# A recurrent branch without GpSimd, and two selection rounds and two rows of a modulation moved by a stage

## The chip, the cores and the metric

The kernel runs on one core of a Trainium2 chip, as one program from inputs in HBM to outputs in HBM. The metric is device time in microseconds of that core, median of several runs. The engines are named as the profile names them: PE (matrix multiplication), DVE (vector), ACT (activations, and copies with scale and bias), POOL (GpSimd), SP (issues most of the DMAs). Each engine runs its own instruction list strictly in order, and semaphores tie the lists together.

## What is computed

Two blocks of a small model on 512 tokens of width 1024, in float32. Only the first block is touched. Cut to what matters:

```
proj = modulate(rmsnorm(h)) @ w_in                      # all projections
xr, gr, q, ckv, qi, ki, wi, mg = split(proj)
hr  = rg_lru(causal_dwconv(xr))                         # 10 blocks of 128 channels
  r, i = sigmoid(x @ w_a + b_a), sigmoid(x @ w_x + b_x)
  log_a = -8 * softplus(-lam) * r;   a = exp(log_a)
  inp = sqrt(-expm1(2 * log_a)) * (i * x)
  h_t = a_t * h_(t-1) + inp_t                           # scan over the tokens
y_a = (gelu(gr) * hr) @ w_rnn_out
sel = top_k(indexer scores, 128 keys for each query);  att = softmax over sel
y_b = att @ w_att_out
mix = (ga * y_a + gb * y_b) @ w_out                     # ga, gb = sigmoid(mg)
h = h + g1 * mix;  u2 = modulate(rmsnorm(h), sh2, sc2)
h = h + g2 * hier_moe(u2)                               # 32 experts
# g1, sh2, sc2, g2: four rows of 1024 of silu(c) @ w_mod + b_mod
```

## The kernel before

Activations are kept feature-major: a tile is 128 channels by 512 tokens. Float32 products are made of three passes on PE: each operand is split into a rounded part (a cast on ACT, L145) and the remainder (a subtraction on DVE, L146), and `mmk` issues high by low, low by high and high by high (L298, L299, L301). `FM.tile` loads 256 columns of a weight matrix (`raw`), splits them into `wh` and `wl`, and multiplies. A split thus needs ACT and then DVE before PE can begin.

A list scheduler decides the order of each engine's instructions from the order of the code, and `weave` interleaves the code of several generators: each is advanced in proportion to the number beside it. Tiles come from pools with a fixed number of buffers.

The stages of the first block that the change touches, with their place in the trace:

- The recurrence (86 to 306 us). `rg_lru` goes over ten blocks of 128 channels in five groups of two. `rg_first` computes the convolution (L691 on ACT, three L693 on DVE) and splits the result (`xcp`); `rg_gates` multiplies it by two gate matrices (`rga`, `rgx`) and multiplies the input gate by x on GpSimd (L709); `rg_decay` makes the decay `a` of a group and the factor of its input out of a sigmoid and a tanh (L717 to L730); `rg_last` applies the square root by one Newton step (L736 to L739), scans (L741), and multiplies by gelu(gr) into `gT`. Beside it run the scores of the key selection (`index_scores`, L623 on ACT and L626 to L630 on DVE) and the first 8 of 16 rounds of `top_k`: in each round and each of three query tiles, a maximum of eight (L636) and their replacement (L637), on DVE.
- Branch A (306 to 373 us): eight tiles of `gT` by `w_rnn_out`, beside the other 8 rounds of `top_k` and row 0 of the second modulation. A row (`mod_rows`) is eight loads of 512 KB, eight multiply-accumulates of 128x1024 on DVE (L802, L804), two small products on PE (L812) and two small additions.
- Attention (373 to 541 us), beside rows 1 to 3 and the last gates.
- Branch B (541 to 592 us): eight tiles of `att` by `w_att_out`, each multiplied by its gate on DVE (L977), added to branch A's on GpSimd (L978) and split into `mT`.
- Then the mix by `w_out`, routing (to 665 us), and the experts (665 to 1122 us), whose weights come by DMA.

Of the kernel before, what the change touches and what calls it, by code (L numbers as in the profile page):

```python
# [64 lines left out]
def build(ctx, tc, I, out, dbg=None):  # L65
# [20 lines left out]
    def weave(*streams):  # L86

        live = [[g, n, 0] for g, n in streams]
        while live:
            s = min(live, key=lambda e: e[2] / e[1])  # L90
            s[2] += 1
            try:
                next(s[0])
            except StopIteration:
                live.remove(s)

    def pipelined(n, score, out, steps=4):

        late = None
        for h in range(n + 1):
            for i in range(steps):
                if h < n:
                    score(h, i)
                if h:
                    products = out(h - 1, i)
                    rest = late and late()
                    late = products
                    if rest:  # L110
                        late = lambda a=rest, b=products: (a(), b())[1]
                yield
        while late:
            late = late()
# [50 lines left out]

    shiftc = const("shiftc", [128, 1])
    G.memset(shiftc, -SHIFT)

    def columns(specs, tag):
        rows = t_([128, 128], F32, "SG", f"rows{tag}")  # L170
# [428 lines left out]
    ps = trp("wit")  # L599
# [15 lines left out]
    def index_scores():  # L615
        for i in range(1, 4):
            n = 128 * (i + 1)
            a = sel[i]
            for h in range(8):
                ps = trp("idx")  # L620
                mm_stacked(ps[:, 0:n], qiT[h // 2], kiT[:, h % 2, 0:n], h % 2, slice(i * 128, (i + 1) * 128))
                rl = sa("rel", n)
                S.activation(rl, ps[:, 0:n], AF.Relu)  # L623
                w = wi[:, i * 8 + h:i * 8 + h + 1]
                if h == 0:
                    V.tensor_scalar(a, rl, w, None, OP.mult)  # L626
                else:
                    V.scalar_tensor_tensor(a, rl, w, a, OP.mult, OP.add)
                yield
            V.tensor_tensor(a[:, i * 128:n], a[:, i * 128:n], cmask, OP.add)  # L630

    def top_k(r0, r1):
        for r in range(r0, r1):
            for i in range(1, 4):
                m8 = sm("m8", 8)
                V.max(m8, sel[i])  # L636
                V.match_replace(sel[i], m8, sel[i], -3e38)  # L637
                yield
        if r1 == 16:
            for i in range(1, 4):  # L640
                V.tensor_scalar(sel[i], sel[i], -1e38, NEG, OP.is_gt, OP.mult)
# [57 lines left out]
    def rg_gates(b, w2, xc, y, keep):  # L699
        wh, wl = w2[:, 0], w2[:, 1]  # L700
        pr = trp("rga")
        mm3(pr, (wh[:, 0], wl[:, 0]), (xc[:, 0], xc[:, 1]), True, True)
        pi = trp("rgx")
        mm3(pi, (wh[:, 1], wl[:, 1]), (xc[:, 0], xc[:, 1]), True, True)
        tx = pt_("tx", F32)
        t, gx = tx[:, 0], tx[:, 1]
        S.activation(t, pr, AF.Sigmoid, bias=col["b_rg_a"][:, b:b + 1])
        S.activation(gx, pi, AF.Sigmoid, bias=col["b_rg_x"][:, b:b + 1])
        G.tensor_tensor(gx, gx, y, OP.mult)  # L709
        keep.append((b, t, gx))  # L710

    def rg_decay(keep):

        ap = pt_("ra", F32)
        for n, (b, t, gx) in enumerate(keep):
            a = ap[:, n]
            S.activation(a, t, AF.Sigmoid, bias=shiftc, scale=sp8[:, b:b + 1])  # L717
            S.activation(a, a, AF.Copy, bias=0.5, scale=0.5 * math.exp(SHIFT))
            S.activation(t, t, AF.Tanh, scale=sp4[:, b:b + 1])
            G.tensor_scalar(t, t, -1e-24, None, OP.min)  # L720
            rec = sg("rec")
            V.scalar_tensor_tensor(rec, t, 1.0, a, OP.subtract, OP.mult)
            V.scalar_tensor_tensor(rec, rec, 2.0, a, OP.add, OP.mult)
            V.tensor_scalar(a, rec, 2.0, -1.0, OP.mult, OP.add)
            G.tensor_tensor(gx, gx, rec, OP.mult)

        ys = []
        for b, t, gx in keep:
            y = sa("rsq")
            S.activation(y, t, AF.Abs_reciprocal_sqrt, scale=-0.25)  # L730
            ys.append(y)
        return [(b, ap[:, n], t, gx, ys[n]) for n, (b, t, gx) in enumerate(keep)]

    def rg_last(b, a, u, gx, y):

        G.tensor_tensor(u, u, y, OP.mult)  # L736
        V.tensor_tensor(y, u, y, OP.mult)
        V.scalar_tensor_tensor(u, y, 12.0, u, OP.add, OP.mult)
        V.scalar_tensor_tensor(gx, u, -1.0 / 16, gx, OP.mult, OP.mult)  # L739
        hs = sg("hs")  # L740
        V.tensor_tensor_scan(hs, a, gx, 0.0, OP.mult, OP.add)  # L741
        ps = fmg.tile(1280 + 128 * b)
        g2 = sg("g2")
        S.activation(g2, ps, AF.Square, scale=math.sqrt(0.044715))
        V.scalar_tensor_tensor(g2, g2, 1.0, ps, OP.add, OP.mult)
        S.activation(g2, g2, AF.Tanh, scale=math.sqrt(2.0 / math.pi))
        V.scalar_tensor_tensor(g2, g2, 1.0, ps, OP.add, OP.mult)
        V.tensor_tensor(g2, g2, hs, OP.mult)
        p = pg("gT")
        split(p[:, 0], p[:, 1], g2)  # L750
        gT.append(p)

    def rg_lru():
        prev = []
        for g in range(6):
            keep = []
            for n in range(2):
                if g < 5:
                    gates = rg_first(2 * g + n, keep)
                    yield  # L760
                    gate(2 * g + n)
                    yield
                if prev:
                    rg_last(*prev[n])
                    yield
                if g < 5:
                    gates()
            if g < 5:
                prev = rg_decay(keep)
                yield  # L770

    def chain(*gs):
        for g in gs:
            yield from g

    weave((rg_lru(), 36), (chain(index_scores(), top_k(0, 8)), 50))


    A_d = dr.tile([8, 128, 512], F32, name="A_d")
# [2 lines left out]
    def branch_a():  # L782
        for d in range(8):
            th = sg("ga")
            load(th, gate_d[d])
            pya = fmy.tile(128 * d)
            V.tensor_tensor(th, th, pya, OP.mult)
            load(A_d[d], th)
            yield
# [1 line left out]

    mod_d = dr.tile([4, 1024], F32, name="mod_d")

    def mod_rows(m0, m1):
        for m in range(m0, m1):
            a = pt_("macc", F32, (128, 1024))
            c0 = 2048 + m * 1024
            for k in range(8):
                raw = pg("raw", F32, (128, 1024))
                load(raw, w_mod[k * 128:(k + 1) * 128, c0:c0 + 1024])  # L800
                if k == 0:
                    V.tensor_scalar(a, raw, csil[:, 0:1], None, OP.mult)  # L802
                else:
                    V.scalar_tensor_tensor(a, raw, csil[:, k:k + 1], a, OP.mult, OP.add)  # L804
                if k % 2:
                    yield
            for hf in range(2):
                cs = slice(hf * 512, hf * 512 + 512)
                br = sg("bmr", 512)
                load(br[0:1, :], I["b_mod"][:, c0 + hf * 512:c0 + hf * 512 + 512])  # L810
                ps = trp("mrow")
                PE.matmul(ps[0:1, :], ones[:, 0:1], a[:, cs], start=True, stop=True)  # L812
                V.tensor_tensor(br[0:1, :], br[0:1, :], ps[0:1, :], OP.add)
                if m == 2:
                    ng = sg("n2g", 512)
                    load(ng[0:1, :], I["norm2_g"][:, cs])
                    V.scalar_tensor_tensor(br[0:1, :], br[0:1, :], 1.0, ng[0:1, :], OP.add, OP.mult)
                load(mod_d[m:m + 1, cs], br[0:1, :])
            yield

    weave((branch_a(), 8), (top_k(8, 16), 24), (mod_rows(0, 1), 6))


    columns(R2, "2")
# [138 lines left out]
            split(p[:, 0], p[:, 1], po)  # L963
            att.append(p)

    weave((pipelined(8, att_score, att_out), 36), (gate_b(), 6), (mod_rows(1, 4), 13))


    fmb = FM(I["w_att_out"][0], att, 0, 1024)
    mT = []  # L970
    for d in range(8):
        ps = fmb.tile(128 * d)
        a = sg("A")
        load(a, A_d[d])
        v = sg("mv")
        load(v, gate_d[8 + d])
        V.tensor_tensor(v, v, ps, OP.mult)  # L977
        G.tensor_tensor(v, v, a, OP.add)  # L978

        p = pg("mT")  # L980
        hi, lo = (p[:, n].rearrange("p (c r) -> p r c", r=8) for n in range(2))
        split(hi, lo, v.rearrange("p (r c) -> p r c", r=8))
        mT.append(p)


    def row(name, src, pinned=False):
        t = pg(name, F32, (128, 1024))
# [1016 lines left out]
```

## Time and profile before

| what | value |
|---|---|
| median of 3 runs | 3099.02 us (3095.4 to 3099.54) |
| profiled execution | 3100.77 us |
| its span in the trace | 3098.6 us |
| PE busy | 2908.0 us, 94% |
| DVE busy | 1840.3 us, 59% |
| ACT busy | 1131.2 us, 37% |
| POOL busy | 279.1 us, 9% |

The span is the time from the first to the last recorded event; the rest of the profiled execution, 2.2 us, lies around it. Busy shares are averages over stages with different limits.

### The profile page before, as it was taken

How to read it: one execution, taken by the hardware profiler on the slowest of the kernel's cores; microseconds unless marked ns; L12 is line 12 of the kernel's file. 1: busy time of each engine (PE TensorE's matmuls, PEld its weight loads, DVE VectorE, ACT ScalarE, POOL GpSimd, SP SyncE). 2: the span in 40 equal slices, each digit the busy share in tenths (PEclk: the TensorE clock that was granted, in tenths of full speed). 3: DMA queues.
4: the chain of work that ended last, by engine and by line, in shares of the span. 5: the costliest groups of instructions: out<-in, count | busy, mean ns of one | idle time of the engine just before them, and what ended most of it. 6: DMA issues, size and time to landing. Idle time of an engine off the chain costs nothing.

```text
span 3098.6 us, 36572 instructions
## 1 busy us (share of the span) xinstructions
PE 2908.0 (94%) x13749; PEld 2192.0 (71%) x13749; DVE 1840.3 (59%) x3521; ACT 1131.2 (37%) x1986; POOL 279.1 (9%) x263
## 2 busy tenths in 40 slices
PE   6988999979999989999999999999999999999998
PEld 5767777743333337888877888888878876788887
DVE  6899978543332347555788644425555589764434
ACT  4555244211000114444666322223444577432221
POOL 2133000310000001211002100000121000200000
PEclk9989999989999999999999999999999999999999
DMA  7222655769999984332244523334433233632341
GB/s 226 94 84 70 218 198 176 260 259 410 411 409 410 409 344 126 116 119 87 69 122 144 203 95 109 106 125 129 126 116 96 75 109 116 228 109 88 103 143 61
DMA packets 291648, 534.17 MB, mean 172 GB/s; under 512 B 29766, under 2 KB 172276, under 8 KB 287366
## 3 DMA queue, kind: packets, MB, share of 16 engines
q1 hardware_dynamic: 288872, 527.45, 48.9%
q0 software_dynamic: 2304, 4.20, 0.4%
q8 instruction: 110, 1.80, 0.2%
q14 instruction: 76, 0.62, 0.1%
q10 hardware_dynamic: 286, 0.09, 0.0%
HBM read 486.50 MB, written 44.38 MB: 171 GB/s over the span
## 4 chain that ended last, share of the span: by engine, by line
PE 57%; DMA 10%; DVE 6%; issue 3%; ACT 2%; POOL 1%; SPq 0%; DVEq 0%; POOLq 0%; ACTq 0%
PE fm L298 9%; PE fm L301 9%; PE fm L299 9%; DMA w<-in_moe_w_dram 6%; PE e L1385 5%; DMA w2r<-in_moe_w_dram 3%; PE ffo L301 2%; PE ffo L298 2%; PE ffo L299 2%; PE mix L298 1%; PE mix L299 1%; PE mix L301 1%; POOL tl L1660 1%; DVE wl L146 1%; PE cmb L1311 1%
## 5 line engine op out<-in xcount | busy, mean ns | idle before, releaser
L146 DVE TENSOR_TENSOR wl<-raw,wh 128x1024 fp32r<-128x1024 f32 (+3 forms) x403 | 461.8, 1147 | 317.2 <-ACT wh L145 315.8
L145 ACT CAST wh<-raw 128x1024 fp32r<-128x1024 f32 (+3 forms) x403 | 388.5, 966 | 546.5 <-PE fm L301 219.5
L298 PE MATMUL fm<-xT,wh 128*128 128x512 f32 (+1 forms) x1264 | 483.5, 385 | 0.0
L299 PE MATMUL fm<-xT,wl 128*128 128x512 f32 (+1 forms) x1264 | 481.4, 383 | 1.3 <-DVE wl L146 1.3
L301 PE MATMUL fm<-xT,wh 128*128 128x512 f32 (+1 forms) x1264 | 302.2, 381 | 0.0
L299 PEld LDWEIGHTS fm<-xT,wl 128*128 128x128 f32 x1264 | 239.5, 189 | 46.8 <-DVE wl L146 1.7
L298 PEld LDWEIGHTS fm<-xT,wh 128*128 128x128 f32 x1264 | 239.3, 189 | 45.2
L1385 PE MATMUL e<-w,xx 128*64 128x512 f32 x1024 | 256.8, 600 | 10.9 <-DMA w<-in_moe_w_dram 10.9
L301 PEld LDWEIGHTS fm<-xT,wh 128*128 128x128 f32 x1264 | 232.0, 188 | 45.6
L1385 PEld LDWEIGHTS e<-w,xx 128*64 128x64 f32 x1024 | 74.9, 137 | 157.9 <-issue 133.0
L1315 DVE TENSOR_TENSOR h<-h,cmb 128x512 f32<-128x512 f32 x128 | 80.7, 682 | 126.5 <-PE cmb L1314 126.1
L299 PE MATMUL fm<-uT,wl 128*128 128x512 f32 (+1 forms) x360 | 144.8, 402 | 3.8 <-DVE wl L146 3.8
L298 PE MATMUL fm<-uT,wh 128*128 128x512 f32 (+1 forms) x360 | 144.4, 402 | 0.0
L298 PE MATMUL ffo<-wl,hid 128*128 128x512 f32 x352 | 137.1, 390 | 0.0
L299 PE MATMUL ffo<-wh,hid 128*128 128x512 f32 x352 | 136.9, 389 | 0.0
L1385 PE MATMUL e<-w2r,hp 128*64 128x512 f32 x512 | 115.1, 596 | 10.1 <-ACT hp L1429 10.1
L1947 DVE SCALAR_TENSOR_TENSOR ffs<-ffs,fm 128x512 f32<-128x512 f32 x44 | 30.2, 687 | 139.3 <-ACT ffs L1946 139.3
L301 PE MATMUL ffo<-wh,hid 128*128 128x512 f32 x352 | 108.4, 389 | 0.0
L1949 DVE SCALAR_TENSOR_TENSOR ffs<-ffs,fm 128x512 f32<-128x512 f32 x44 | 30.2, 687 | 114.4 <-PE fm L301 114.4
L1660 POOL TENSOR_TENSOR tl<-ml,tl 128x512 f32<-128x512 f32 x32 | 47.7, 1496 | 555.1 <-DVE tl L1656 550.3
L1946 ACT ACTIVATE ffs<-fm 128x512 f32<-128x512 f32 x44 | 26.3, 598 | 188.7 <-PE fm L301 188.7
L1385 PEld LDWEIGHTS e<-w2r,hp 128*64 128x64 f32 x512 | 41.1, 136 | 73.1 <-issue 58.9
(603 smaller groups left out, 5938.0 us busy)
## 6 DMA issues: line engine op xcount, KB each, us to landing
w<-in_moe_w_dram SPq DMA_DIRECT2D x192, 512.0 KB
raw<-in_w_in_dram SPq DMA_DIRECT2D x71, 1024.0 KB
w2r<-in_moe_w_dram SPq DMA_DIRECT2D x128, 512.0 KB
raw<-in_w_ffn_in_dram SPq DMA_DIRECT2D x44, 1024.0 KB
w<-in_moe_w_dram SPq DMA_DIRECT2D x32, 1024.0 KB
raw<-in_w_mod_dram SPq DMA_DIRECT2D x42, 512.0 KB
raw<-in_w_ffn_out_dram SPq DMA_DIRECT2D x20, 1024.0 KB
raw<-in_w_out_dram SPq DMA_DIRECT2D x12, 1024.0 KB
```

The lines of the kernel that those rows point to most:

```text
L145: S.copy(hi, src)
L146: (eng or V).tensor_tensor(lo, src, f(hi), OP.subtract)
L298: PE.matmul(ps, l[0], r[1], start=start and n == 0, stop=False)
L299: PE.matmul(ps, l[1], r[0], start=False, stop=False)
L301: PE.matmul(ps, l[0], r[0], start=False, stop=stop and n == len(pairs) - 1)
L1311: mm = PE.matmul(ps, pl, yl[:, cs], start=True, stop=False)
L1315: V.tensor_tensor(h1[i][m], h1[i][m], ps, OP.add)
L1385: mm = PE.matmul(ps[hs], lhs[:, hs], rhs[h], start=start, stop=stop)
L1660: G.tensor_tensor(th, m, th, OP.add)
L1946: S.activation(s, pgt, AF.Tanh, scale=0.5)
L1947: V.scalar_tensor_tensor(s, s, 1.0, pgt, OP.add, OP.mult)
L1949: V.scalar_tensor_tensor(s, s, 0.5, pup, OP.mult, OP.mult)
```

## The change

In the recurrence four kinds of instructions leave GpSimd. Three products of 128x512 per block (L709, L725, L736) go to DVE. The clamp `min(t, -1e-24)` (L720) is dropped, and a constant bias of 2.5e-25 inside the reciprocal square root (L730) keeps its argument from zero in its place. The last step of the decay, `a = 2 rec - 1` (L724), goes from DVE to ACT. Of the 16 rounds of `top_k` 6 are written in the recurrence and 10 in branch A, where it was 8 and 8. Row 0 of the second modulation is written in the attention (with rows 2 and 1), and row 3 in branch B. There the addition of branch A's part (L978) goes from GpSimd to DVE.

```diff
+    tinyc = const("tinyc", [128, 1])
+    G.memset(tinyc, 2.5e-25)
...
-        G.tensor_tensor(gx, gx, y, OP.mult)
+        V.tensor_tensor(gx, gx, y, OP.mult)
         keep.append((b, t, gx))
...
             S.activation(t, t, AF.Tanh, scale=sp4[:, b:b + 1])
-            G.tensor_scalar(t, t, -1e-24, None, OP.min)
             rec = sg("rec")
             V.scalar_tensor_tensor(rec, t, 1.0, a, OP.subtract, OP.mult)
             V.scalar_tensor_tensor(rec, rec, 2.0, a, OP.add, OP.mult)
-            V.tensor_scalar(a, rec, 2.0, -1.0, OP.mult, OP.add)
-            G.tensor_tensor(gx, gx, rec, OP.mult)
+            S.activation(a, rec, AF.Copy, bias=-1.0, scale=2.0)
+            V.tensor_tensor(gx, gx, rec, OP.mult)
...
-            S.activation(y, t, AF.Abs_reciprocal_sqrt, scale=-0.25)
+            S.activation(y, t, AF.Abs_reciprocal_sqrt, bias=tinyc, scale=-0.25)
...
-        G.tensor_tensor(u, u, y, OP.mult)
+        V.tensor_tensor(u, u, y, OP.mult)
...
-    weave((rg_lru(), 36), (chain(index_scores(), top_k(0, 8)), 50))
+    weave((rg_lru(), 36), (chain(index_scores(), top_k(0, 6)), 44))
...
-    def mod_rows(m0, m1):
-        for m in range(m0, m1):
+    def mod_rows(*rows):
+        for m in rows:
...
-    weave((branch_a(), 8), (top_k(8, 16), 24), (mod_rows(0, 1), 6))
+    weave((branch_a(), 8), (top_k(6, 16), 30))
...
-    weave((pipelined(8, att_score, att_out), 36), (gate_b(), 6), (mod_rows(1, 4), 13))
+    weave((pipelined(8, att_score, att_out), 36), (gate_b(), 6), (mod_rows(0, 2, 1), 15))
...
-        G.tensor_tensor(v, v, a, OP.add)
+            V.tensor_tensor(v, v, a, OP.add)
...
+    weave((branch_b(), 8), (mod_rows(3), 5))
```

The line numbers after the change are higher by 2 from L709 on and by 4 in branch B (L722 is L723, L723 is L724, L724 is L725 on ACT, L725 is L726, L736 to L741 are L738 to L743, L978 is L982).

On DVE, at the decay of the second group (`rec` is the decay's intermediate, `tx` holds the two gates, `ra` the decay, `rsq` the reciprocal root), the list before is:

```order
L722 SCALAR_TENSOR_TENSOR rec_1367<-tx_1203,ra_1362 128x512
L934 SCALAR_TENSOR_TENSOR bm_3162<-selp_734,cmask 128x128
L723 SCALAR_TENSOR_TENSOR rec_1367<-rec_1367,ra_1362 128x512
L722 SCALAR_TENSOR_TENSOR rec_1376<-tx_1358,ra_1362 128x512
L724 TENSOR_SCALAR ra_1362<-rec_1367 128x512
L723 SCALAR_TENSOR_TENSOR rec_1376<-rec_1376,ra_1362 128x512
L724 TENSOR_SCALAR ra_1362<-rec_1376 128x512
L737 TENSOR_TENSOR rsq_1381<-tx_1203,rsq_1381 128x512
L626 TENSOR_SCALAR selp_734<-rel_1389,wi 128x512
L738 SCALAR_TENSOR_TENSOR tx_1203<-rsq_1381,tx_1203 128x512
L146 TENSOR_TENSOR rgh_1395<-rgw_1392,rgh_1395 128x256
L739 SCALAR_TENSOR_TENSOR tx_1203<-tx_1203 128x512
```

And after the change:

```order
L723 SCALAR_TENSOR_TENSOR rec_1354<-tx_1191,ra_1350 128x512
L724 SCALAR_TENSOR_TENSOR rec_1354<-rec_1354,ra_1350 128x512
L723 SCALAR_TENSOR_TENSOR rec_1362<-tx_1346,ra_1350 128x512
L726 TENSOR_TENSOR tx_1191<-tx_1191,rec_1354 128x512
L724 SCALAR_TENSOR_TENSOR rec_1362<-rec_1362,ra_1350 128x512
L738 TENSOR_TENSOR tx_1191<-tx_1191,rsq_1367 128x512
L726 TENSOR_TENSOR tx_1346<-tx_1346,rec_1362 128x512
L739 TENSOR_TENSOR rsq_1367<-tx_1191,rsq_1367 128x512
L738 TENSOR_TENSOR tx_1346<-tx_1346,rsq_1369 128x512
L630 SCALAR_TENSOR_TENSOR selp_735<-rel_1374,wi,selp_735 128x384
L146 TENSOR_TENSOR rgh_1380<-rgw_1377,rgh_1380 128x256
L695 SCALAR_TENSOR_TENSOR xc_1414<-fm_1385,cols_104,xc_1414 128x509
```

The three products (L726, L738) now stand between the steps of the decay, and the two L724 of before are gone from this engine. From the first `rec` row up to the subtraction that ends the next block's `xcp` there are 20 rows before and 19 now.

On ACT, at the same place, before (`wh` and `rgh` are the casts of weights for PE):

```order
L719 ACTIVATE tx_1358<-tx_1358,sp_791 128x512
L730 ACT_TABLE_LOAD
L730 ACTIVATE rsq_1381<-tx_1203 128x512
L730 ACTIVATE rsq_1383<-tx_1358 128x512
L623 ACTIVATE rel_1389<-idx_1386 128x512
L145 CAST wh_1560<-raw_1398 128x1024
L145 CAST rgh_1395<-rgw_1392 128x256
```

After:

```order
L721 ACTIVATE tx_1346<-tx_1346,sp_793 128x512
L732 ACT_TABLE_LOAD
L732 ACTIVATE rsq_1367<-tx_1191,tinyc 128x512
L725 ACTIVATE ra_1350<-rec_1354 128x512
L725 ACTIVATE ra_1350<-rec_1362 128x512
L732 ACTIVATE rsq_1369<-tx_1346,tinyc 128x512
L625 ACTIVATE rel_1374<-idx_1371 128x384
L145 CAST rgh_1380<-rgw_1377 128x256
```

Two copies (L725) that read DVE's `rec` now stand ahead of the second root and of the casts.

On PE, where the recurrence ends and branch A begins (`fm` is an output tile of branch A, `gT` its input; in each list the last two `gT` are the blocks that finish last), before:

```order
L298 MATMUL fm_2478<-gT_2184,wh_2498 128x512
L299 MATMUL fm_2478<-gT_2184,wl_2499 128x512
L298 MATMUL fm_2478<-gT_2330,wh_2498 128x512
L299 MATMUL fm_2478<-gT_2330,wl_2499 128x512
L299 MATMUL fm_2537<-gT_1180,wl_2539 128x512
L298 MATMUL fm_2537<-gT_1335,wh_2538 128x512
L299 MATMUL fm_2537<-gT_1335,wl_2539 128x512
L298 MATMUL fm_2537<-gT_1532,wh_2538 128x512
L299 MATMUL fm_2537<-gT_1532,wl_2539 128x512
L298 MATMUL fm_2537<-gT_1687,wh_2538 128x512
```

After:

```order
L300 MATMUL fm_2452<-gT_2166,wh_2472 128x512
L301 MATMUL fm_2452<-gT_2166,wl_2473 128x512
L300 MATMUL fm_2452<-gT_2306,wh_2472 128x512
L301 MATMUL fm_2452<-gT_2306,wl_2473 128x512
L300 MATMUL fm_2452<-gT_2394,wh_2472 128x512
L301 MATMUL fm_2452<-gT_2394,wl_2473 128x512
L300 MATMUL fm_2452<-gT_2441,wh_2472 128x512
L301 MATMUL fm_2452<-gT_2441,wl_2473 128x512
L303 MATMUL fm_2452<-gT_1993,wh_2472 128x512
L303 MATMUL fm_2452<-gT_2166,wh_2472 128x512
```

Before, rows of the next tile that need only the first blocks' `gT` (`fm_2537`) stand behind the third `gT`; now the rows that need the last two blocks (`gT_2394`, `gT_2441`) stand there, and the next tile behind them.

On SP, in the middle of branch B after the change (`mv` and `A` are the gate and branch A's part of a tile, `raw` loads weights):

```order
L980 DMA mv_4765<-gate_d 128x512
L978 DMA A_4809<-A_d 128x512
L980 DMA mv_4811<-gate_d 128x512
L402 DMA raw_4993<-in_w_out_dram 128x4x512
L978 DMA A_4853<-A_d 128x512
L402 DMA raw_5055<-in_w_out_dram 128x4x512
L802 DMA raw_4772<-in_w_mod_dram 128x1024
L802 DMA raw_4775<-in_w_mod_dram 128x1024
L802 DMA raw_4818<-in_w_mod_dram 128x1024
L802 DMA raw_4821<-in_w_mod_dram 128x1024
L980 DMA mv_4855<-gate_d 128x512
L978 DMA A_4893<-A_d 128x512
```

Four of the eight loads of row 3 (`in_w_mod`) now stand behind two loads of `w_out` and ahead of the sixth tile's `mv`; before, all loads of the rows stood ahead of the second tile's `mv`.

## Rows read from the trace of the kernel before

**Rows 1.** The windows by stage: us, busy of each engine, granted clock, DMA share, GB/s.

```profile
86.00:306.00 220.00, 197.25 (x834) 160.84 (x833) 194.22 (x316) 124.52 (x189) 66.68 (x40) 0.94 0.27 84
306.00:373.00 67.00, 57.34 (x236) 44.73 (x235) 62.50 (x119) 15.30 (x21) 1.02 (x4) 0.95 0.71 225
373.00:541.00 168.00, 159.64 (x798) 128.43 (x797) 139.81 (x343) 71.48 (x153) 0.00 (x0) 0.98 0.54 183
541.00:592.00 51.00, 46.22 (x191) 36.00 (x190) 29.69 (x34) 17.45 (x17) 17.62 (x11) 0.97 0.66 205
640.00:665.00 25.00, 8.40 (x83) 7.62 (x83) 12.15 (x59) 3.65 (x7) 2.19 (x2) 0.66 0.37 125
665.00:1122.00 457.00, 436.66 (x1880) 173.54 (x1882) 149.72 (x231) 44.19 (x75) 14.18 (x14) 1.00 1.02 408
```

**Rows 2.** The chain of waits, 86 to 313 us: us in total, times, longest.

```profile
PE rga L298 <- DVE xcp L146: 15.8, 3, 6.5
...
PE fm L299 <- DVE wl L146: 8.9, 3, 5.9
...
DVE rec L722 <- POOL tx L720: 7.6, 5, 4.1
...
PE rga L298 <- ACT rel L623: 3.9, 1, 3.9
```

**Rows 3.** The groups on DVE, 86 to 313 us: busy, mean ns, idle before.

```profile
L724 DVE TENSOR_SCALAR ra<-rec 128x512 f32<-128x512 f32 x10 | 12.9, 1295 | 0.1
...
L723 DVE SCALAR_TENSOR_TENSOR rec<-rec,ra 128x512 f32<-128x512 f32 x10 | 12.3, 1228 | 0.0
...
L737 DVE TENSOR_TENSOR rsq<-tx,rsq 128x512 f32<-128x512 f32 x10 | 11.2, 1117 | 0.0
...
L722 DVE SCALAR_TENSOR_TENSOR rec<-tx,ra 128x512 f32<-128x512 f32 x10 | 9.5, 954 | 7.6 <-POOL tx L720 7.6
```

**Rows 4.** The single lines, whole run: shortest/median/longest ns, first and last start.

```profile
L724 DVE TENSOR_SCALAR ra<-rec x10: 426/1508/1522, 117.7 to 305.4; 128x512 f32<-128x512 f32 x10
...
L723 DVE SCALAR_TENSOR_TENSOR rec<-rec,ra x10: 675/1232/1780, 116.5 to 303.1; 128x512 f32<-128x512 f32 x10
...
L748 DVE TENSOR_TENSOR g<-g,hs x10: 672/678/1094, 138.7 to 318.6; 128x512 f32<-128x512 f32 x10
...
L718 ACT ACTIVATE ra<-ra x10: 616/623/636, 112.5 to 296.6; 128x512 f32<-128x512 f32 x10
...
L636 DVE MAX8 m<-selp x48: 405/544/686, 134.0 to 364.2; 128x8 f32<-128x256 f32 x16, 128x8 f32<-128x384 f32 x16, 128x8 f32<-128x512 f32 x16
...
L637 DVE MATCH_REPLACE8 selp<-m,selp x48: 398/540/678, 141.4 to 365.6; 128x256 f32<-128x256 f32 x16, 128x384 f32<-128x384 f32 x16, 128x512 f32<-128x512 f32 x16
...
L804 DVE SCALAR_TENSOR_TENSOR macc<-raw,csil,macc x28: 1270/1278/2141, 326.9 to 548.4; 128x1024 f32<-128x1024 f32 x28
...
L978 POOL TENSOR_TENSOR mv<-mv,A x8: 1283/2048/2742, 545.0 to 587.0; 128x512 f32<-128x512 f32 x8
```

**Rows 5.** The timeline of DVE, second group: start, us, instruction.

```profile
161.78 1.09 DVE L722 SCALAR_TENSOR_TENSOR rec<-tx,ra 128x512 f32<-128x512 f32 x1 [1.68 <-POOL tx L720]
...
162.99 0.68 DVE L723 SCALAR_TENSOR_TENSOR rec<-rec,ra 128x512 f32<-128x512 f32 x1
...
163.59 0.68 DVE L722 SCALAR_TENSOR_TENSOR rec<-tx,ra 128x512 f32<-128x512 f32 x1
...
178.67 0.67 DVE L146 TENSOR_TENSOR xcp<-xc,xcp 128x512 fp32r<-128x512 f32 x1
```

**Rows 6.** The timeline of PE, ends of two gaps.

```profile
179.39 0.79 PE L298 MATMUL rga<-xcp,rgh 128*128 128x512 f32 x1 [6.46 <-DVE xcp L146]
...
312.41 0.79 PE L299 MATMUL fm<-gT,wl 128*128 128x512 f32 x1 [5.86 <-DVE wl L146]
```

**Rows 7.** The window behind the gap that ends at 179.39 us.

```profile
179.39:183.90 4.51, 4.51 (x11) 3.54 (x12) 4.51 (x7) 1.89 (x3) 0.78 (x1) 0.50 0.92 282
```

**Rows 8.** The chain of waits of PE, 541 to 592 us.

```profile
PE mix L298 <- DVE mv L977: 3.6, 1, 3.6
```

More of the change, by code (lines that the diff above doesn't have):

```diff
@@ L964, in att_products, with branch_b @@
             att.append(p)
-    weave((pipelined(8, att_score, att_out), 36), (gate_b(), 6), (mod_rows(1, 4), 13))
+    weave((pipelined(8, att_score, att_out), 36), (gate_b(), 6), (mod_rows(0, 2, 1), 15))
     fmb = FM(I["w_att_out"][0], att, 0, 1024)
     mT = []
[L971 to L977, printed above, removed]
-        G.tensor_tensor(v, v, a, OP.add)
[L980 to L983, printed above, removed]
+    def branch_b():
+        for d in range(8):
+            ps = fmb.tile(128 * d)
+            a = sg("A")
+            load(a, A_d[d])
+            v = sg("mv")
+            load(v, gate_d[8 + d])
+            V.tensor_tensor(v, v, ps, OP.mult)
+            V.tensor_tensor(v, v, a, OP.add)
+            p = pg("mT")
+            hi, lo = (p[:, n].rearrange("p (c r) -> p r c", r=8) for n in range(2))
+            split(hi, lo, v.rearrange("p (r c) -> p r c", r=8))
+            mT.append(p)
+            yield
+    weave((branch_b(), 8), (mod_rows(3), 5))
     def row(name, src, pinned=False):
```

## The prediction

> **What bounds the kernel now.** I read the windows by stage first [rows 1]. In the recurrence PE is busy 197.3 of 220 us and DVE 194.2: both nearly full, and the question is who waits for whom at the joints. ACT has 124.5 us and POOL 66.7. In branch A it is the same at DVE 62.5 of 67. In the attention PE is the bound (159.6 of 168). Branch B leaves DVE 21 us idle. The experts are bound by DMA (share 1.02, 408 GB/s): they begin when the work before them is done, and the DMA share just ahead of them is 0.37, so time won before 640 us should survive: nothing there is on a fixed transfer that would already be running.
>
> The chain of waits says where PE stands still [rows 2]: 15.8 us in three waits for `xcp` from DVE, 8.9 in three for a weight's split from DVE, 3.9 in one for ACT. Together 28.6 us. The reader is to see that these are few and long (up to 6.5 us), so they belong to places: behind the decays of the five groups, two of them in two pieces. The timeline of PE shows two of them, ending at 179.39 and at 312.41 us [rows 6]. And PE comes back slow: in the 4.51 us behind the first of these the granted clock is 0.50, the lower of its two levels (1.2 GHz), so 2.25 us more are lost there [rows 7]. Five such places at that price are 11.3 us. PE could win 28.6 + 11.3 = 39.9 us at the very most.
>
> Why is DVE late at a decay? Its own instructions stretch. L724 takes 426 ns at best and 1508 in the median, L723 675 ns at best and 1232 in the median [rows 4]; a same-sized product away from POOL's work (L748) takes 678 in the median. And DVE waits 7.6 us in all for POOL's clamp, L720 [rows 2].
>
> **What the change costs and frees on DVE, in the recurrence.**
> - L724 leaves: 10 x 1.295 = 12.9 us [rows 3].
> - With no work left on POOL beside them, L723 falls from 1.228 to 0.675 (5.5 us for ten), L737 from 1.117 to 0.678 (4.4) and L722 from 0.954 to 0.678 (2.8): 12.7 us [rows 3, 4]. I take the shortest or undisturbed duration because POOL has nothing left to run in this stage; the bound below is nothing, if the stretching had another cause.
> - Selection rounds: a round is three maxima and three replacements, 405 + 544 + 686 and 398 + 540 + 678 ns, 3.25 us [rows 4]. The code moves two rounds, but the scheduler moves more: of the 48 rows of L636, 30 stand ahead of the last scan before and 18 now. That is four rounds, 13.0 us.
> - Three products come in, 30 x 0.678 = 20.3 us at L748's price.
>
> The sum is -12.9 - 12.7 - 13.0 + 20.3 = -18.3 us of work, and 7.6 us of waiting for L720 besides. The rounds stand where the scheduler finds room, not in the decay's chain; without them a group's chain is shorter by (12.9 + 12.7 + 7.6 - 20.3) / 5 = 2.6 us.
>
> **The gaps one by one.** The second group I work out by rows. Before, from the first `rec` (161.78) to the start of the subtraction `xcp` (178.67) there are 16.9 us [rows 5]. Now 19 rows stand in that stretch, at the spacing of two undisturbed neighbours (162.99 to 163.59, 0.60 us) 11.4 us. It also begins 1.68 us earlier, the wait for L720. That is 7.2 us earlier, and the gap is 6.46 [rows 6]: it closes, 6.5 us.
>
> The last gap, 5.86 us, I leave as it is. In PE's order the rows that need the last two blocks now stand straight behind the third block's, and the next tile's rows, with which PE filled this time before, stand behind them. The shorter chain of DVE is used up by that.
>
> The other three hold 28.6 - 6.5 - 5.9 = 16.2 us. From below they win 3 x 2.6 = 7.8 us, from above all 16.2, if the deferred rounds make the room. One of them waits for ACT, so I stay near the lower end: 10 us. Gaps together: 16.5 us.
>
> The clock: where a gap closes, the slow stretch behind it should go too. I count two of the five, 2 x 2.25 = 4.5 us [rows 7]; bounds 0 and 11.3.
>
> **ACT.** Ten copies come, at the price of the like copy L718 0.623 us [rows 4], 6.2 us on an engine that is idle 95 us in this stage: nothing, while they don't wait. They stand in order ahead of casts that PE needs. The second reads a `rec` that DVE ends four rows after the second `tanh`, 2.4 us at 0.60 each; ahead of it on ACT are a table load and a root that take about as long. So 0, with a rival below; a cast that came late by one copy in each group would cost 5 x 0.6 = 3 us, the bound above. The bias adds no instruction.
>
> There is a rule that speaks against this step. The Trainium skill, Perfetto Trace Analysis, section Optimizing Scalar/DVE Operations, says that where DVE has a faster mode for an operation it is the better engine, and that offloading pays only if DVE is saturated. The trace agrees as to the bare durations: 426 ns on DVE at best against 623 for L718 on ACT [rows 4]. By the rule the step would have stayed on DVE at 4.3 us for ten, 0.9 a group: with POOL silent a group's chain would then be shorter by 1.7 us and not by 2.6, the lower bound for three gaps 5.1 and not 7.8, the sum some 3 us less, and ACT would wait for nothing. The move is worth these 3 us only as long as rival 4 doesn't come.
>
> **Branch A.** DVE gets the four rounds (+13.0) and loses row 0 (8 x 1.278 = 10.2, small parts left out) [rows 4]: +2.8 us where 4.5 are idle [rows 1]. 0, bounds 0 and +2.8. PE waits elsewhere anyway.
>
> **Attention.** Three rows before, three now. 0.
>
> **Branch B.** Eight additions come to DVE, 8 x 0.678 = 5.4 us, and row 3's eight steps, 10.2 us at most, since some of row 3 already ran here (L804's last start is 548.4 [rows 4]). 29.7 + 15.6 = 45.3 of 51 us: fits, but tightly. In return the addition takes 0.68 instead of 2.05 us (L978), and the 3.6 us that PE waits for the last tile [rows 8] could shrink by 1.4. Row 3's 4 MB are 10.3 us at 408 GB/s; the stage's DMA share is 0.66, which leaves 17 us. I take 0, bounds -1.4 and +5.
>
> **Sum.** 16.5 + 4.5 = 21 us. The profiled execution, 3100.8, becomes 3079.8; it stands 1.75 us over the median, so 3078.
>
> **Rivals.**
> 1. *Little is won* (7 to 14 us, 3085 to 3092). The gaps shrink only by the second group's 6.5 us and the lower price of the others (7.8), and the clock gives nothing back. For it: without the rounds DVE's work falls by 5.3 us only, and DVE stays as full as PE. Against: the second gap closes by more than its length.
> 2. *PE reaches its floor* (33 to 40 us, 3059 to 3066). All gaps but the last close (22.7) and the clock is given back in all five places (11.3): 34 us. For it: the deferred rounds are 13 us of slack at the right time. Against: branch A must take them with 4.5 us idle.
> 3. *Given back in branch B* (same, 3093 to 3105). Four loads of row 3 stand on SP's queue behind two loads of `w_out`, and if those wait for buffers, DVE waits in its L804 rows with `mv` of the sixth tile queued behind. Row 3's transfers one after another cost 10.3 us, and the 10.2 us of steps follow: up to 20 us lost, against the 21. For it: the order. Against: DMA has 17 us free, and before the same loads lay beside the same work.
> 4. *Slower* (over 3105). The copy L725 waits on ACT for DVE's `rec`, and the casts behind it (`rgh`, `wh`) come late, so that PE starves behind each decay. To end 6 us slower it must eat 27 us over five groups, 5.4 us a group. For it: DVE may still be in other rows when the `tanh` comes, as an engine that is full. Against: 2.4 us of DVE rows to the second `rec`; a wait of 5.4 would need nine rows of 0.60 more than stand there.
>
> **Chances.** The forecast (gain 15 to 32 us) 0.48, rival 1 0.17, rival 2 0.12, rival 3 0.13, rival 4 0.10. 0.2% (6.2 us) is about what a measurement can tell from no change. Faster are the forecast and rivals 1 and 2: 0.77; the same 0.13; slower 0.10. The range takes in rivals 1 and 2, with 2 us to spare at the lower end for terms that I left at 0, and the near edge of 3: 3057 to 3096. The likeliest case alone would have 3067 to 3084.
>
> **What would show it.** POOL empty from 86 to 306 us; L723 and its like at 0.68 with no 1.78 among them; L725 on ACT at 0.62 with waits for `rec` under 1 us; the gap behind the second decay gone, the one near 306 us still 5 to 8 us; 18 maxima ahead of the last scan; the experts' window as long as before and about 21 us earlier. The prediction is wrong if DVE's instructions stay stretched with POOL empty, if casts wait behind L725, or if DVE in branch B waits for row 3 in front of `mv`.

## The result, and the profile after

The changed kernel takes 3060.14 us (median of 4 runs, 3058.39 to 3061.85) against 3099.28 beside it; the ratio is 0.9874, 95% interval 0.986 to 0.9888. That is 39.1 us, inside the range (3057 to 3096) but nearly twice the forecast's 21: the time is that of rival 2, PE at its floor, which had a chance of 0.12. Measured once more, it took 3062.03 us against 3096.17 beside it, 34.1 less (ratio 0.9883, 0.9866 to 0.99).

The first two views are windows cut in both kernels where PE begins the next step: the first product of the scores, of branch A, of the attention, of `w_att_out`, of the routing, of the experts. The first window holds the same products in both, and so do the other four taken together; in the middle three some products change window, the rows' small ones and some of the attention's. Columns as in [rows 1]. Before:

```profile
88.90:302.50 213.60, 190.85 (x805) 155.61 (x804) 188.05 (x306) 122.01 (x186) 63.81 (x38) 0.94 0.27 85
302.50:383.90 81.40, 71.75 (x310) 56.94 (x310) 74.72 (x155) 21.78 (x31) 3.90 (x6) 0.96 0.65 204
383.90:526.20 142.30, 135.53 (x674) 108.81 (x674) 120.13 (x291) 62.93 (x136) 0.00 (x0) 0.98 0.51 176
526.20:626.70 100.50, 93.87 (x411) 74.41 (x410) 62.84 (x92) 28.90 (x38) 27.81 (x18) 0.98 0.75 251
626.70:665.00 38.30, 17.11 (x167) 14.83 (x167) 24.02 (x86) 6.20 (x13) 4.07 (x4) 0.78 0.54 183
```

And after:

```profile
88.80:273.30 184.50, 181.85 (x805) 149.16 (x804) 168.97 (x296) 126.59 (x196) 0.00 (x0) 1.00 0.31 99
273.30:349.00 75.70, 69.79 (x307) 56.42 (x307) 69.93 (x166) 22.06 (x31) 0.44 (x3) 0.95 0.51 163
349.00:490.10 141.10, 133.39 (x666) 107.10 (x666) 121.97 (x301) 62.33 (x135) 0.00 (x0) 0.96 0.54 189
490.10:587.80 97.70, 95.23 (x422) 74.36 (x420) 75.29 (x111) 30.66 (x39) 12.03 (x10) 1.00 0.82 286
587.80:626.20 38.40, 17.07 (x166) 14.80 (x167) 24.07 (x86) 6.20 (x13) 4.07 (x4) 0.79 0.54 182
```

Read the first line of each. The same 805 products take 29.1 us less: PE's idle time falls from 22.75 (213.60 - 190.85) to 2.65 us, and its busy time by 9.0 us, because the granted clock is 1.00 on the mean and was 0.94. Branch A gives 5.7 us, the attention 1.2, branch B with the mix 2.8, routing nothing: 38.7 us up to the experts. The rest of the program takes 2433.6 and 2431.0 us in this pair of executions, which differ by 41.8 us in all.

PE's waits from 86 to 290 us, which answer to [rows 2]:

```profile
PE fm L300 <- DVE gT L146: 4.4, 2, 3.4
PE fm L301 <- DVE wl L146: 4.1, 4, 1.5
```

No wait for `xcp` or for ACT is left. Three short waits for a weight's split (1.03, 0.42 and 1.17 us, ending at 207.34, 219.08 and 243.71 us) are all that is left of the idle time in the recurrence's window; the other 5.9 us are the last gap, which lies behind the first product of branch A in both kernels and so in branch A's window.

The groups of DVE that answer to [rows 3], where L723, L724 and L739 were L722, L723 and L737, and one of the products that came from GpSimd (L738). None is stretched any more:

```profile
L738 DVE TENSOR_TENSOR tx<-tx,rsq 128x512 f32<-128x512 f32 x10 | 6.9, 687 | 0.0
L723 DVE SCALAR_TENSOR_TENSOR rec<-tx,ra 128x512 f32<-128x512 f32 x10 | 6.9, 687 | 1.8 <-ACT tx L721 1.8
L724 DVE SCALAR_TENSOR_TENSOR rec<-rec,ra 128x512 f32<-128x512 f32 x10 | 6.9, 685 | 0.1
L739 DVE TENSOR_TENSOR rsq<-tx,rsq 128x512 f32<-128x512 f32 x10 | 6.8, 681 | 0.0
```

DVE's timeline in the second group, which answers to [rows 5]; from the first `rec` to `xcp` there are 10.89 us where there were 16.89:

```profile
153.04 0.69 DVE L723 SCALAR_TENSOR_TENSOR rec<-tx,ra 128x512 f32<-128x512 f32 x1
...
163.93 0.68 DVE L146 TENSOR_TENSOR xcp<-xc,xcp 128x512 fp32r<-128x512 f32 x1
```

And ACT's there. The two copies (L725, 1.14 us together) and the casts behind them follow one another without a wait:

```profile
155.45 0.73 ACT L732 ACTIVATE rsq<-tx,tinyc 128x512 f32<-128x512 f32 x1
156.08 1.14 ACT L725 ACTIVATE ra<-rec 128x512 f32<-128x512 f32 x2
157.12 0.71 ACT L732 ACTIVATE rsq<-tx,tinyc 128x512 f32<-128x512 f32 x1
157.74 0.47 ACT L625 ACTIVATE rel<-idx 128x384 f32<-128x384 f32 x1
158.11 0.39 ACT L145 CAST rgh<-rgw 128x256 fp32r<-128x256 f32 x1
```

### The profile page after: what moved, and what is told of

It reads as the page before. It is cut to its first block, busy times and chain, and to the rows that moved or that the text cites. A ratio compares the mean times of both kernels' runs of the same rounds, so it can differ in the third digit from the quotient of the medians.

```text
span 3057.2 us, 36511 instructions
## 1 busy us (share of the span) xinstructions
PE 2893.9 (95%) x13749; PEld 2181.7 (71%) x13749; DVE 1832.8 (60%) x3549; ACT 1137.3 (37%) x1996; POOL 196.3 (6%) x216
## 4 chain that ended last, share of the span: by engine, by line
PE 56%; DMA 11%; DVE 6%; issue 3%; ACT 2%; POOL 1%; SPq 0%; DVEq 0%; POOLq 0%; ACTq 0%
PE fm L303 9%; PE fm L300 9%; PE fm L301 9%; DMA w<-in_moe_w_dram 7%; PE e L1391 4%; DMA w2r<-in_moe_w_dram 3%; PE ffo L303 2%; PE ffo L300 2%; PE ffo L301 2%; PE mix L300 1%; PE mix L301 1%; PE mix L303 1%; POOL tl L1666 1%; DVE wl L146 1%; DMA tl<-t_d 1%
## 5 line engine op out<-in xcount | busy, mean ns | idle before, releaser
L1307 DVE SCALAR_TENSOR_TENSOR y<-e,gts,g2R 128x512 f32<-128x512 f32 x32 | 22.9, 748 | 116.3 <-PE e L1391 116.0
```

Of the source, the lines that this page charges most:

```text
L1307: V.scalar_tensor_tensor(y[:, cs], py[m], gtc, g2R[:, cs], OP.mult, OP.mult)
```

## The experiments

Two theories for where the recurrence's time came from. **A:** GpSimd was the delay; its instructions stood in the chain of each decay and stretched DVE's. **B:** DVE lacked room, and the rounds that went to branch A made it. Beside the median (the kernel before, beside each, took 3096.17 to 3099.28 us), the table has two figures from each trace: the time from the first `rec` of a group to the next `xcp` on DVE (first four groups), and the time from the first product of the scores to the first product of the experts. The second is the sharper one: the part behind it, 2431 to 2439 us, varies from kernel to kernel though no instruction of it is touched. Two profiles of the changed kernel differ by 1.6 us in it.

| kernel | median us | `rec` to `xcp`, us | scores to experts, us |
|---|---|---|---|
| before | 3099.28 | 15.8 to 16.9 | 576.1 |
| changed | 3060.14 | 10.9 to 11.8 | 537.4 |
| changed, once more | 3062.03 | 10.9 to 11.8 | 539.0 |
| engines_only | 3074.40 | 10.2 to 11.0 | 550.4 |
| schedule_only | 3092.81 | 14.7 to 16.3 | 571.3 |
| idle_pool | 3070.18 | 12.1 to 13.3 | 546.5 |
| products_on_pool | 3077.56 | 14.7 to 16.3 | 555.2 |
| clamp_back | 3068.41 | 10.7 to 12.2 | 544.4 |
| step_on_dve | 3066.83 | 9.5 to 10.7 | 540.6 |
| rounds_back | 3065.66 | 10.2 to 11.0 | 541.9 |
| rounds_4_12 | 3058.61 | 10.3 to 13.0 | 535.2 |
| rows_back | 3075.37 | as changed | 549.6 |
| rows_attention | 3070.68 | as changed | 545.7 |
| add_on_pool | 3068.62 | as changed | 545.4 |

**Engines alone, and schedule alone.** The first takes the kernel before and changes the lines of the recurrence as the diff does; the second takes the changed kernel and puts GpSimd back:

```diff
-            S.activation(a, rec, AF.Copy, bias=-1.0, scale=2.0)
+            V.tensor_scalar(a, rec, 2.0, -1.0, OP.mult, OP.add)
...
-            V.tensor_tensor(gx, gx, rec, OP.mult)
+            G.tensor_tensor(gx, gx, rec, OP.mult)
```

(the other two products, the clamp and branch B's addition likewise).

> The kernel before with the change of engines in the recurrence alone (three products to DVE, the clamp dropped, the last step of the decay on ACT); the rounds 8 and 8, the four rows and branch B as before. Theory A (GpSimd was the delay: its instructions stood in the chain of each decay and stretched those of DVE): all of what the recurrence won comes from here, the four gaps before 280 us close, 3066 to 3074 us. Theory B (room on DVE was the delay, and the later rounds made it): at most half, 3080 to 3090 us, with gaps of 3 us and more left in the third and fourth group.

> The changed kernel with the engines of before (products, clamp and the addition of branch B on GpSimd, the last step of the decay on DVE); rounds 6 and 10 and the rows one stage later as changed. Theory A: only what branch A and the later stages won, 6 to 10 us, 3089 to 3093 us, and the gaps in the recurrence stay within 5 us of the 22.7 before. Theory B: 18 to 25 us won, 3074 to 3081 us.

Engines alone: 3074.40 us, ratio 0.9927 (0.9905 to 0.9948). Schedule alone: 3092.81, ratio 0.9981 (0.997 to 0.9992). PE's waits in the recurrence, engines alone:

```profile
PE fm L301 <- DVE wl L146: 11.9, 3, 10.0
PE rga L300 <- DVE xcp L146: 0.8, 2, 0.7
```

Schedule alone:

```profile
PE rga L300 <- DVE xcp L146: 18.1, 4, 6.1
PE fm L301 <- DVE wl L146: 7.2, 2, 6.2
```

With the engines changed, the gaps for `xcp` are gone but for 0.8 us, though 24 maxima stand ahead of the last scan; with the schedule changed, four of up to 6.1 us stay, though only 23 do. That is theory A.

The two parts win 24.2 and 5.7 us (against the runs of before beside them, 3098.55), 30 together, where the whole change wins 34 to 39; in the last column of the table it is 25.7 and 4.8 against 37.1 to 38.7. The surplus does not come from the recurrence or branch A. From the scores to the attention it is 295.0 us before, 268.3 with the engines alone, 284.2 with the schedule alone and 260.2 with both: 26.7 and 10.8 us apart, and only 34.8 together. It comes from branch B with the mix, where it was 100.50 us before and is 97.70 with both. Engines alone, then schedule alone:

```profile
500.20:602.70 102.50, 94.95 (x410) 75.11 (x409) 61.93 (x92) 28.97 (x38) 27.46 (x18) 0.97 0.74 246
```

```profile
513.20:620.00 106.80, 98.43 (x422) 75.56 (x420) 73.48 (x103) 29.81 (x39) 28.28 (x18) 0.97 0.75 261
```

Schedule alone has row 3 there and the addition on GpSimd, and loses 6.3 us in this stage; its longest wait is for row 3's small product:

```profile
PE mrow L815 <- DVE macc L807: 5.9, 2, 5.4
```

The last experiment below shows the same wait with nothing but the addition put back.

**Idle work on GpSimd.** What GpSimd costs others, apart from its own time in the chain. The added products change no output:

```diff
+    dtrig = const("dtrig", [128, 10])
+    dwork = const("dwork", [128, 128])
+    G.memset(dwork, 1.0)
...
+            S.copy(dtrig[:, b:b + 1], t[:, 0:1])
+            G.tensor_copy(dwork[:, 0:1], dtrig[:, b:b + 1])
+            for _ in range(16):
+                G.tensor_tensor(dwork, dwork, dwork, OP.mult)
             rec = sg("rec")
```

> The changed kernel with useless work on GpSimd beside each decay: 16 products of 128x128 on a tile of its own per block, started by the tanh, that nothing waits for. Theory A1 (GpSimd's reads stretch DVE's instructions): DVE's two-input instructions beside it grow from 0.68 to over 1 us on the mean, some 10 us are lost, 3066 to 3076 us. Theory A2 (only the time of GpSimd's own instructions in the chain counted): 3059 to 3063 us, the same as the changed kernel.

3070.18 us, 8 to 10 more than the changed kernel in its two measurements, 7.5 to 9.1 up to the experts. Three groups of this kernel, where L731 is the second step of the decay and L745 a product that came from GpSimd (0.69 us each in the changed kernel); the last is the idle work:

```profile
L745 DVE TENSOR_TENSOR tx<-tx,rsq 128x512 f32<-128x512 f32 x10 | 8.2, 816 | 0.0
...
L731 DVE SCALAR_TENSOR_TENSOR rec<-rec,ra 128x512 f32<-128x512 f32 x10 | 7.5, 745 | 0.1
```

```profile
L728 POOL TENSOR_TENSOR dwork<-dwork 128x128 f32<-128x128 f32 x136 | 96.2, 707 | 10.7
```

A1 holds in its direction: nothing waits for this work (ACT has ten small copies more, which start it), and each group's stretch from `rec` to `xcp` is 0.3 to 2.1 us longer, with 19 or 20 rows in it where the changed kernel has 19. The size per instruction was too high: the mean grows by 0.06 to 0.13 us and not to over 1 us. These GpSimd instructions of 0.71 us stretch less than those of before (means of 1.6 to 2.0 us), beside which L723 took up to 1.78 us [rows 4]; whether their length is the reason was not tested.

**The products back on GpSimd; the clamp back.**

```diff
-        V.tensor_tensor(gx, gx, y, OP.mult)
+        G.tensor_tensor(gx, gx, y, OP.mult)
```

(and the same in L726 and L738); the other kernel only adds the line `G.tensor_scalar(t, t, -1e-24, None, OP.min)` again.

> The changed kernel with its three products (L711, L726, L738) on GpSimd again; the clamp stays dropped and the last step of the decay on ACT. Theory A: the chain of a decay has two instructions of GpSimd of about 1.6 us again and DVE is stretched again, 3072 to 3085 us. Theory B (DVE's work decides): DVE has 20 us less to do, the same or faster than the changed kernel, 3052 to 3062 us.

> The changed kernel with the clamp of the tanh on GpSimd again (1.5 us, between the tanh and both the first step of the decay and the root); all else as changed. Theory A (every instruction of GpSimd in the chain counts by its time): each decay begins 1.5 us or more later, gaps of 1 us come back behind the decays, the end of the recurrence is 3 to 8 us later, 3064 to 3069 us. Theory B (only the products counted): within 3 us of the changed kernel.

With the products back 16.1 to 17.8 us are lost up to the experts: the stretch from `rec` to `xcp` is nearly that of before, and DVE waits for GpSimd inside it, although it has 20 us less to do:

```profile
DVE rsq L739 <- POOL tx L738: 9.0, 4, 2.7
PE fm L301 <- DVE wl L146: 7.9, 2, 4.5
PE rga L300 <- DVE xcp L146: 6.3, 3, 2.7
```

With the clamp back it is 5.4 to 7.0 us; DVE waits at the first step of the decay, as it did before [rows 2], and PE has a gap of 1.6 us for `xcp` and one of 2.9 for a split in the recurrence:

```profile
DVE rec L724 <- POOL tx L722: 8.3, 5, 3.5
```

**The last step of the decay on DVE.**

```diff
-            S.activation(a, rec, AF.Copy, bias=-1.0, scale=2.0)
+            V.tensor_scalar(a, rec, 2.0, -1.0, OP.mult, OP.add)
```

> The changed kernel with the last step of the decay on DVE (L724 of before), GpSimd still empty. If DVE is quicker for it and ACT's copies wait: the instruction takes 0.43 us, 0.9 us more of DVE for each group, ACT's casts come 1.2 us earlier; the same as the changed kernel within 3 us, 3057 to 3063 us. If DVE's list sets the time in the recurrence: 4.3 us more, 3062 to 3066 us.

The instruction takes 0.42 us there:

```profile
L725 DVE TENSOR_SCALAR ra<-rec x10: 415/420/421, 114.8 to 272.7; 128x512 f32<-128x512 f32 x10
```

3066.83 us (3061.93 to 3070.01). Up to the experts it is 1.6 to 3.2 us longer than the changed kernel, as 4.2 us more on a full DVE would have it; the rest of the median's distance lies behind, in the part that varies. The stretch from `rec` to `xcp` is even shorter (9.5 to 10.7 us), so the order of the list differs too. Quicker for the instruction, not for the kernel; the size is near what two profiles differ by.

**Rounds: 8 and 8 again, and 4 and 12.**

```diff
-    weave((rg_lru(), 36), (chain(index_scores(), top_k(0, 6)), 44))
+    weave((rg_lru(), 36), (chain(index_scores(), top_k(0, 8)), 50))
...
-    weave((branch_a(), 8), (top_k(6, 16), 30))
+    weave((branch_a(), 8), (top_k(8, 16), 24))
```

(4 and 12 with the weights 38 and 36.)

> The changed kernel with the selection rounds 8 and 8 again; engines and rows as changed. Theory A (the rounds don't matter while the engines are freed, other than at the end of the recurrence, where six maxima with their replacements, 3.3 us or so more for a full round, stand in DVE's list ahead of the last block): the gaps of the first four groups stay closed, the last one is near 10 us as in the kernel with the engines alone, 3063 to 3068 us. Theory B (room): gaps of 2 us and more in the third and fourth group, 3068 to 3075 us.

> The changed kernel with 4 selection rounds in the recurrence and 12 in branch A. If the last gap of the recurrence hangs on the maxima that stand in DVE's list at the end: a millisecond's thousandth or two less there, 3057 to 3060 us. If branch A, where DVE has 18 of 67 us left, is then the bound: 3061 to 3066 us.

8 and 8 cost 2.9 to 4.5 us up to the experts, all at the end of the recurrence: the wait there is 9.96 us, and the four gaps before it stay closed. My reason, maxima ahead of the last block, was wrong: its decay begins at 264.75 us, earlier than in the changed kernel. The timelines show what PE waits for. With 8 and 8, the split of a weight (128x1024) stands on DVE behind the last decay, and PE waits for it:

```profile
277.87 1.22 DVE L146 TENSOR_TENSOR wl<-raw,wh 128x1024 fp32r<-128x1024 f32 x1
```

```profile
279.14 0.79 PE L301 MATMUL fm<-uT,wl 128*128 128x512 f32 x1 [9.96 <-DVE wl L146]
```

In the changed kernel the split of that weight, the last of this size (at 263.54), stands ahead of the last decay (first `rec` at 267.21), and PE goes on into branch A until its next split and the last `gT` stop it:

```profile
263.54 1.22 DVE L146 TENSOR_TENSOR wl<-raw,wh 128x1024 fp32r<-128x1024 f32 x1
...
267.21 0.69 DVE L723 SCALAR_TENSOR_TENSOR rec<-tx,ra 128x512 f32<-128x512 f32 x1
```

```profile
278.83 0.50 PE L301 MATMUL fm<-gT,wl 128*128 128x512 f32 x1 [1.48 <-DVE wl L146]
...
283.67 0.79 PE L300 MATMUL fm<-gT,wh 128*128 128x512 f32 x1 [3.40 <-DVE gT L146]
```

The 10.0 us of engines alone are the same wait. Why the scheduler places the split there was not looked into. 4 and 12 is 3.4 us faster than the changed kernel beside it on the chip (3057.82 to 3059.74 against 3060.57 to 3062.45), and 2.2 to 3.8 us up to the experts: the best kernel here, by less than 0.2%. Branch A with its twelve rounds takes as long as with ten (75.7 us), so DVE was not the bound there. The 18 of 67 us in that expectation, and the 154 of 168 in the one on the rows beside the attention, were read from the changed kernel at the times of before, where other stages lie in it; DVE is busy for 69.93 of 75.70 us in its branch A and for 121.97 of 141.10 in its attention.

**Rows: as before; all beside the attention. The addition back on GpSimd.**

```diff
-    weave((pipelined(8, att_score, att_out), 36), (gate_b(), 6), (mod_rows(0, 2, 1), 15))
+    weave((pipelined(8, att_score, att_out), 36), (gate_b(), 6), (mod_rows(0, 2, 1, 3), 20))
...
-    weave((branch_b(), 8), (mod_rows(3), 5))
+    weave((branch_b(), 8))
```

(The other two: `(mod_rows(0), 6)` beside branch A and `(mod_rows(1, 2, 3), 13)` beside the attention; and `G` for `V` in L982.)

> The changed kernel with the four rows where they were: row 0 beside branch A, rows 1 to 3 beside the attention, none in branch B. Theory A (row 0 made branch A DVE-bound, and taking it out won the 6 us of that stage): branch A is 5 to 7 us longer, branch B 1 to 3 us shorter, 3063 to 3067 us. Theory B (the row only moves its cost to the other stages): 3058 to 3062 us, the same.

> The changed kernel with all four rows beside the attention (0, 2, 1, 3), none in branch B; branch A and the recurrence as changed. If row 3 costs nothing where it stands: DVE, at 154 of 168 us in the attention, is loaded by 11 us more, 3062 to 3072 us. If row 3 holds up branch B: branch B is 3 us shorter and the total the same, 3058 to 3062 us.

> The changed kernel with branch B's addition (L982) on GpSimd again. Theory A (branch B's end hangs on the last tile's chain of product, addition and split): PE's wait at the first product of the mix grows by the 1.4 us between 2.05 and 0.68, 3061 to 3064 us. Theory B (the order of tiles and loads decides there): within 1.5 us of the changed kernel.

Rows as before cost 10.6 to 12.2 us, more than either theory. Windows of that kernel in branch A and the attention, with the same ends as above:

```profile
275.10:360.60 85.50, 75.82 (x311) 58.54 (x309) 78.78 (x169) 21.92 (x31) 0.63 (x3) 0.92 0.57 187
360.60:506.00 145.40, 135.64 (x673) 107.66 (x673) 121.54 (x308) 62.65 (x136) 0.00 (x0) 0.96 0.51 176
```

Branch A is 85.50 us against 75.70 and 76.40 in the two profiles of the changed kernel, the attention 145.40 against 141.10 and 142.10; the clock in branch A is 0.92 against 0.95 and 0.93. Why the attention is longer too, with three rows in either kernel, was not found out. All rows beside the attention cost 6.7 to 8.3 us, in the attention alone:

```profile
352.60:501.40 148.80, 136.72 (x667) 107.62 (x667) 128.39 (x304) 60.70 (x132) 0.00 (x0) 0.97 0.56 200
501.40:598.90 97.50, 93.94 (x421) 75.08 (x419) 69.41 (x106) 31.85 (x41) 12.05 (x10) 1.00 0.75 254
```

Branch B with the mix takes 97.50 us here without row 3, 95.60 in the kernel with the rows as before, and 97.70 with row 3: the row costs 0.2 to 2.1 us there. The addition on GpSimd costs 6.4 to 8.0 us, some five times what I gave it. The waits there show that PE's largest is not for the last tile:

```profile
ACT mT L145 <- POOL mv L982: 28.3, 7, 7.3
...
DVE mT L146 <- ACT mT L145: 10.4, 7, 2.7
...
PE mrow L814 <- DVE macc L806: 5.9, 2, 5.4
...
PE mix L300 <- DVE mv L981: 1.2, 1, 1.2
```

Row 3's small product stands in PE's list and waits for DVE; DVE, in order, waits for splits (`mT`) that wait for GpSimd's additions. With row 3 in branch B, the addition is better off on DVE, by these 6.4 to 8.0 us.

## Why the prediction was right, and where its size was off

**The bound and the place: right.** PE waited at joints for a DVE that was late behind each decay, and GpSimd made it late. DVE's busy time fell from 188.05 to 168.97 us, 19.1; the ledger said 18.3. L723 and its like are at 0.68 to 0.69 us. But 13.0 of the ledger's 18.3 us were the deferred rounds, on which my upper bound for the gaps hung, and they were not needed: engines alone, with the rounds 8 and 8, closes the four gaps as well.

**The other three gaps: 10 us, measured 13.6.** Of their 16.2 us the waits for `xcp` and ACT closed whole, and 2.6 stay in the short waits for a split. This term was too small by its method. For the second group I counted the rows between `rec` and `xcp` and got 11.4 us; it is 10.9. For the others I spread DVE's ledger over five groups, 2.6 us each, and stayed near that. But the ledger has DVE's work, and the chain has GpSimd's time as well. The count of the list held for all four: each stretch is 4 to 6 us shorter, and each decay begins without the clamp's wait (1.8 us are left of 7.6, for a tanh). The clamp back alone, and the products back alone, bring gaps again.

**The clock: 4.5 us, measured 9.0.** I let it come back behind two of the five gaps. It came back behind all four that closed: 190.85 us of the same products became 181.85, at a granted clock of 1.00 over the whole window. Four at my price of 2.25 us would be 9.0.

**The last gap: right, by another path.** It is 5.9 us (1.48 + 3.40 + 1.03 in pieces), and that it is the same to a tenth is luck. PE waits for a split and the last two `gT`, as its order said. The experiments add that this place hangs on where the scheduler puts one weight's split, worth 4 us with 8 and 8 rounds (9.96 us).

**Branch A: 0, measured 5.7.** I added DVE's work, found it to fit, and did not ask what PE waits for in this stage. Before, its idle time there is 9.65 us: the last gap's 5.86, two short waits for splits and one for row 0's small product:

```profile
PE fm L299 <- DVE wl L146: 7.9, 3, 5.9
PE mrow L812 <- DVE macc L804: 1.7, 1, 1.7
```

After, the 5.91 us that are left are the last gap alone. The other 2.0 us are busy time, and mostly moved: row 0's small products no longer run here, and branch B has a row's more. The schedule did this and not the engines, since schedule alone takes 75.5 us here with GpSimd as before. Row 0 by itself is worth 3.4 us with eight rounds (from the scores to the attention 268.3 us in engines alone and 264.9 with 8 and 8); put back beside ten rounds it costs 9.1 to 9.8 us in this stage.

**Attention and branch B: 0, measured 1.2 and 2.8.** The two profiles of the changed kernel differ by 1.0 us in the attention, so the 1.2 is hardly more than noise. In branch B the wait for the last tile, 3.6 us [rows 8], from which I took 1.4 at the most, is gone; the longest wait left there is this:

```profile
PE mrow L814 <- DVE macc L806: 1.9, 2, 1.4
```

Rival 3 did not come: DVE has 75.29 of 97.70 us in branch B and the mix, and row 3 costs at most 2.1 us there. That the addition on DVE is what allows it was not in the prediction.

**ACT: right, rival 4 did not come.** The copies take 0.62 us, and ACT does not stand idle in front of any of the ten. The rule of the Trainium skill (Perfetto Trace Analysis, Optimizing Scalar/DVE Operations) agrees with the run as to the instruction, 0.42 us on DVE; that the kernel would be some 3 us the better for it with the step left on DVE was my sum from it, and the run shows no such gain. Its exception, a saturated DVE, is the case here: DVE is busy for 168.97 of 184.50 us.

So 38.7 us are 20.1 of idle time and 9.0 of clock in the recurrence, 5.7 in branch A, 1.2 and 2.8 behind it, less 0.1 in routing. The forecast had 16.5, 4.5, 0, 0 and 0. Rival 2 had 34 us, all in the recurrence, which gave 29.1; the 9.7 behind it, which rival 2 left at nothing too, brought the time into its bounds. So the mechanism was right, and the terms that were too small are the other three gaps, the clock and the stages behind the recurrence.

What stays open: of the four kinds of instructions that left GpSimd, the three products were put back together and only the clamp by itself; how the 16.1 to 17.8 us with the products back divide between waiting for GpSimd and stretched instructions was not separated.

## What to carry to other kernels

Price a slow engine's instruction by the chain that it stands in, not by a ledger of busy time: count the list from the first late instruction to the one that the bounding engine waits for, for every place, and add the slow clock behind each wait. Two parts of a change can be worth more together than apart, and windows by stage show where: here the surplus of 6.6 to 8.2 us came from one stage, in which a row and an addition had been moved, and not from the stage that the change was made for. And after each such change look at what stands in the list just ahead of a joint: one weight's split behind the last decay was worth 4 us.

## What was not expected of the hardware

GpSimd slows DVE even with work that nothing waits for: 136 products of 128x128 in the recurrence, 0.71 us each, raised the means of DVE's decay instructions from 0.68 to between 0.74 and 0.82 us and cost 7.5 to 9.1 us up to the experts, with nearly the same order of DVE's instructions around the decay. How much of this is the decay's and how much that of other stretched instructions was not separated.
